# A hybrid decoder block: the carried attention state multiplied in 64-row pairs

## Chip, cores and metric

The kernel runs on one core of a Trainium2 chip. The metric is the time of one execution on the device in microseconds (us), the median of several runs. The profile comes from one more execution. Engines are called by these names: TensorE (PE in the profile, PEld for its weight loads), VectorE (DVE), ScalarE (ACT), GpSimd (POOL) and SyncE (SP), which issues the transfers. Matrix products land in PSUM, which has eight banks, of 512 fp32 values in each of 128 partitions.

## What is computed

One decoder layer over 2048 positions of width 1024: a norm, one input projection, two mixers side by side (gated linear attention with four heads, and a short gated convolution), an output projection with residual, a norm, a gated feed-forward part with residual, and a last norm. The change touches the attention alone. Per head, with q and k of width 64 and v of width 128:

```python
b = jnp.cumsum(log_a, axis=-2)
b_last = b[..., -1:, :]
q_i = q * jnp.exp(b)
k_i = k * jnp.exp(-b)
k_s = k * jnp.exp(b_last - b)
scores = jnp.einsum('nbhck,nbhsk->nbhcs', q_i, k_i)
scores = jnp.where(causal, scores, 0.0)
o_intra = jnp.einsum('nbhcs,nbhsv->nbhcv', scores, v)
chunk_kv = jnp.einsum('nbhsk,nbhsv->nbhkv', k_s, v)
...
o_inter = jnp.einsum('nbhck,nbhkv->nbhcv', q_i, state_prev)
o = o_intra + o_inter
```

`state_prev` is what all earlier chunks left: after each chunk the state is multiplied by the chunk's decay and `chunk_kv` is added. The output of each head is then normalised over its 128 values. The kernel takes chunks of 128 positions, 16 in all.

## The kernel before

Everything is laid out with features in partitions and positions along the free dimension. The positions are cut into four blocks `b` of 512, and two blocks make a half. The big products (`unit`, lines 332 to 370) work on a half at once in a scheme of seven block products instead of eight; each operand is split into a high and a low part (`split`, lines 145 to 147: ScalarE writes the high one, VectorE the difference), and each product of tiles is three matmuls (`product_step`, lines 328 to 330). One block product is 12 such matmuls into one bank.

The order of the body is: statistics and operands of the first half; input projection of half 0 (`in_proj`); the same of half 1; output projection of both halves (`out_proj`); the feed-forward part of both halves (`ffn_up`, `ffn_down`). The attention is a background job: a generator (`gla_half`, lines 578 to 598) that is put on a list when q, k, v and the gate of its half are projected, and that `tick` (lines 187 to 192) advances by one step behind every second block product. So the program text mixes attention steps between block products. The final order on each engine is then laid out by a planner ahead of the run, from estimated times, in priority of the program text: an instruction whose operands are late by the estimate lets later ones of its engine pass. On the chip each engine keeps the order so made and stands at an instruction whose operands are not there. The program's semaphores are put in by the same framework, and PSUM banks come from one pool of eight (`ps`, line 61), so a new tile waits until a bank is free.

One attention chunk (`b`, `t`) goes through four functions:

- `gla_load` (603 to 615) fetches k, q, decays, v and gate from scratch memory (SyncE issues 14 transfers), ScalarE takes two exponentials (609, 610) and VectorE multiplies them into `kq` (611, 612). `kq[:, 0:2]` holds the keys, `kq[:, 2:4]` the queries; in both, two heads `h = 2*i + e` share the 128 rows of pair `i`, head `e` in rows `64*e` to `64*e + 63`.
- `gla_scores` (617 to 639): four score matmuls of 64 rows, the two heads of a pair into two banks (622); VectorE copies them under the causal mask (625) to `scores`; TensorE transposes the keys into `kt_ps` (628) and the values into `v_ps` (631), ScalarE copies both out (632, 633); ScalarE scales the carried `state` by the chunk's decay `em` into `carry` (638), one head at a time.
- `gla_outputs` (641 to 676): for each head one matmul of scores and values (646) and one of queries and carry (648), added in one bank `o_ps`. The second one takes all 128 rows of the pair; `carry[:, h]` holds zeros in the other head's rows. Then chunk products `kv` of keys and values (653), VectorE's update of `state` (660 to 666), ScalarE's squares for the norm (670), VectorE's small steps (671, 155 to 158) and its scaling of the output (675).
- `gla_finish` (678 to 686) transposes the output (682), multiplies gain and gate (683), splits it and stores it.

In `gla_half` the steps follow each other as: scores of chunk n, finish of chunk n - 1, load of chunk n + 1, outputs of chunk n. The first chunk has no carry, and the last makes no `kv`.

Of the kernel before, what the change touches and what calls it, by code (L numbers as in the profile page):

```python
# [10 lines left out]
F32 = mybir.dt.float32  # L11
F32R = mybir.dt.float32r
U32 = mybir.dt.uint32
AF = mybir.ActivationFunctionType
ALU = mybir.AluOpType
# [3 lines left out]
P = 128  # L19
# [6 lines left out]
HEADS = 4  # L26
# [21 lines left out]
def tile_hymba_block(ctx, tc, x, xt, win, wa, wgu, wout, wffn, wdown, wdown_first, small, out):  # L48
    nc = tc.nc
    act, dve, pool, pe = nc.scalar, nc.vector, nc.gpsimd, nc.tensor  # L50

    def pool_of(name, bufs, **kw):
        return ctx.enter_context(tc.tile_pool(name=name, bufs=bufs, **kw))
# [7 lines left out]
    ps = pool_of("ps", 8, space=PSUM)  # L61
# [3 lines left out]
    mixer = mixing.enter_context(tc.tile_pool(name="mixer", bufs=1))  # L65
# [8 lines left out]
    mask = mixer.tile([P, 2, P], F32, name="mask")  # L74
# [12 lines left out]
    dve.memset(wa_sb[:, KD * 64 :].bitcast(F32), 0.0)  # L87
    scores = mixer.tile([P, HEADS, P], F32, name="scores")
    dve.memset(scores[:], 0.0)
    carry = mixer.tile([P, HEADS, P], F32, name="carry")  # L90
    dve.memset(carry[:], 0.0)
    state = [mixer.tile([P, P], F32, name=f"state{i}") for i in range(2)]
    halo = mixer.tile([P, 4, 2], F32, name="halo")
    dve.memset(halo[:], 0.0)
# [39 lines left out]
    def bt(name, shape=(P, PB)):  # L134
        return bx[0].tile(list(shape), F32, name=name, tag="b")
# [13 lines left out]
    def rsqrt(y, v, l, y0):  # L149

        act.activation(l, v, AF.Ln)
        act.activation(y0, l, AF.Exp, scale=-0.5)
        newton(y, v, l, y0)
# [298 lines left out]
    def build_h(later):  # L452


        def quad(k, j):
            return scaled(col(C_G1 + k), rbs[j], raws[j, k])

        return build_first(quad, first_weights, later)
# [119 lines left out]
    def gla_half(half):  # L578
        chunks = [(b, t) for b in (2 * half, 2 * half + 1) for t in range(PT)]
        with tc.issue_after(last_silu[0].ins):  # L580
            tables = act.preload_act_table_set("natural_log_exp_and_others")
        with tc.issue_after(tables.ins):
            nxt = gla_load(*chunks[0])
        o = None
        for n, (b, t) in enumerate(chunks):
            cur = nxt
            s = gla_scores(b, t, *cur)
            yield
            if o is not None:
                gla_finish(*chunks[n - 1], *o)  # L590
                yield
            if n + 1 < len(chunks):
                nxt = gla_load(*chunks[n + 1])
            o = gla_outputs(b, t, *s)
            yield
        gla_finish(b, t, *o)
        done.add((b, t))
        yield
# [16 lines left out]
        return kq, e, vt, g  # L615

    def gla_scores(b, t, kq, kt, v, g):
        sc = [ps.tile([P, 2, P], F32, name="sc", tag="mm") for _ in range(2)]
        for i in range(2):
            for e in range(2):  # L620
                r = slice(64 * e, 64 * e + 64)
                pe.matmul(sc[e][:, i, :], kq[r, i, :], kq[r, 2 + i, :], start=True, stop=True)
        smv = scores.rearrange("p (i e) c -> p e i c", e=2)
        for e in range(2):
            dve.copy_predicated(smv[:, e], mask[:].bitcast(U32), sc[e][:])
        kt_ps = ps.tile([P, 2, P], F32, name="kt_ps", tag="mm")
        for i in range(2):
            pe.transpose(kt_ps[:, i, :], kq[:, i, :], ident[:])
        v_ps = ps.tile([P, HEADS, P], F32, name="v_ps", tag="mm")
        for h in range(HEADS):  # L630
            pe.transpose(v_ps[:, h, :], v[:, h, :], ident[:])
        act.activation(kt[:, 0:2, :], kt_ps[:], AF.Copy)
        act.activation(v[:], v_ps[:], AF.Copy)
        if b or t:
            em = decays[b][0]
            for h in range(HEADS):
                i, r = h // 2, slice(64 * (h % 2), 64 * (h % 2) + 64)
                act.activation(carry[r, h, :], state[i][r, :], AF.Copy, scale=em[r, i, t : t + 1])
        return kq, kt, v, g

    def gla_outputs(b, t, kq, kt, v, g):
        first = b == 0 and t == 0
        _, dn, el = decays[b]
        o = ps.tile([P, HEADS, P], F32, name="o_ps", tag="mm")
        for h in range(HEADS):
            pe.matmul(o[:, h, :], scores[:, h, :], v[:, h, :], start=True, stop=first)
            if not first:
                pe.matmul(o[:, h, :], kq[:, 2 + h // 2, :], carry[:, h, :], start=False, stop=True)
        if b < NB - 1 or t < PT - 1:
            kv = ps.tile([P, 2, P], F32, name="kv", tag="mm")  # L650
            for i in range(2):
                for e in range(2):
                    pe.matmul(
                        kv[64 * e : 64 * e + 64, i, :], kt[:, i, 64 * e : 64 * e + 64],
                        v[:, 2 * i + e, :], start=True, stop=True,
                    )
            for i in range(2):
                last = el[:, i, t : t + 1]
                if first:
                    dve.tensor_scalar(state[i][:], kv[:, i, :], last, None, ALU.mult)  # L660
                else:
                    kvs = mtiny.tile([P, P], F32, name="kvs", tag="kvs")
                    dve.tensor_scalar(kvs[:], kv[:, i, :], last, None, ALU.mult)
                    dve.scalar_tensor_tensor(
                        state[i][:], state[i][:], dn[:, i, t : t + 1], kvs[:], ALU.mult, ALU.add
                    )
        ssq, l, y0 = [mtiny.tile([P, HEADS], F32, name=n, tag=n) for n in ("hsq", "hl", "hy")]
        sq = mtiny.tile([P, P], F32, name="sq", tag="rep")
        for h in range(HEADS):
            act.activation(sq[:], o[:, h, :], AF.Square, accum_out=ssq[:, h : h + 1])  # L670
        dve.tensor_scalar(ssq[:], ssq[:], 1.0 / P, EPS, ALU.mult, ALU.add)
        rsqrt(ssq[:], ssq[:], l[:], y0[:])
        osb = bt("osb", (P, HEADS, P))
        rs = ssq[:].rearrange("p (h c) -> p h c", c=1).to_broadcast([P, HEADS, P])
        dve.tensor_tensor(osb[:], o[:], rs, ALU.mult)
        return osb, g

    def gla_finish(b, t, osb, g):
# [27 lines left out]
    def build_mix(half):  # L706
        def pair(b, k):
            return load_pair(s_gla[b][:, k] if k < HEADS else s_mix[b][k - HEADS])

        return [[pair(2 * half + j, k) for j in range(2)] for k in range(KD)]  # L710
# [42 lines left out]
    def h2_first(ssq, ops):  # L753


        for _ in range(6):
            yield
        rb = []
        for j in range(2):
            rb.append(tiny.tile([P, PB], F32, name="rb2", tag="rb"))  # L760
            column_rstd(ssq[j], D, rb[j])
            yield

        def put(n, k, h):
            if n in LATER:
                store(s_h2[n][k][:], h[:])
            else:
                ops[n].append(split_op(h[:]))

        yield from combine(lambda k, j: s_x1[j][k][:], C_G2, rb, put)  # L770

    def h2_rest(ops):
        hs = deque()
        order = [(n, k) for n in LATER for k in range(4)]

        def fetch():
            if order:
                n, k = order.pop(0)
                h = bt("h")
                load(h[:], s_h2[n][k][:])  # L780
                hs.append((n, h))

        for _ in range(4):
            fetch()
        while hs:
            for _ in range(2):
                n, h = hs.popleft()
                ops[n].append(split_op(h[:]))
                fetch()
            yield  # L790
# [180 lines left out]
    ops, first = build_h(later)  # L971
# [10 lines left out]
    ssq = out_proj(0, build_mix(0))  # L982
    drain_background(lambda: (3, PT - 1) in done)
    h2 = no_operands()
    ssq = out_proj(1, build_mix(1), h2_first(ssq, h2), h2_rest(h2))
# [115 lines left out]
```

## Time and profile before

| what | us |
|---|---|
| median of three runs | 2149.33 |
| the three runs | 2149.33, 2143.01, 2150.7 |
| the profiled execution | 2146.09 |
| its span, first to last instruction | 2144.2 |
| attention chunks in the span, about | 305 to 700 |

The mean clock granted to TensorE was 0.989 of full speed. In the lines of the profile "L622" is line 622 of the kernel; a group of instructions is written as line, engine, operation, tiles written and read, shape, count, then busy time in us and the mean ns of one, then idle time of the engine ahead of it with the engine that ended it. A line of the timeline is start in us, duration, engine, line, operation, tiles, shape and count of merged instructions, with idle time ahead of it in brackets. A line of the waits is who waits, for whom, the us in total, the times, and the longest. A program matmul of two fp32 operands shows as two MATMUL instructions.

### The profile page before, as it was taken

The page shows a single profiled execution, that of the slowest core. Times are in us where ns is not written, and L with a number is a line of the kernel's source. Part 1 is how long each engine was busy: PE and PEld are TensorE (multiplying, and loading weights), DVE is VectorE, ACT ScalarE, POOL GpSimd, SP SyncE. Part 2 cuts the span into 40 slices and gives each one's busy share as a digit, 9 for nine tenths or more (in the row PEclk, how much of TensorE's full clock was granted, in tenths as well). Part 3 has the DMA queues.
Part 4 walks back from the last instruction along what each step waited for, and adds up shares of the span by engine and source line. Part 5 has one row for each costly group of instructions (what it writes and reads, how often), then busy time and mean ns, then how long its engine had stood idle before and what let it go on. Part 6 is the DMA issues. An engine that isn't in the chain of part 4 may idle for free.

```text
span 2144.2 us, 26906 instructions
## 1 busy us (share of the span) xinstructions
PE 2043.6 (95%) x9133; PEld 1651.3 (77%) x9133; DVE 1452.5 (68%) x2034; ACT 1012.1 (47%) x1962; POOL 997.0 (46%) x714
## 2 busy tenths in 40 slices
PE   4899899999999999999999999999999999999996
PEld 2677687887888887788888887787888888887775
DVE  8849965556774486888887664554686677664554
ACT  4555434574544235555454553333454454553344
POOL 4526422122201274655655436774644654445774
PEclk9999999999999999999999999999999999999998
DMA  4259658532577884465464577689455455487662
GB/s 150 76 199 315 218 228 286 156 125 79 166 247 256 309 294 152 167 240 220 172 237 182 185 303 283 254 336 355 157 191 205 154 197 196 172 329 293 266 265 108
DMA packets 189977, 467.64 MB, mean 218 GB/s; under 512 B 19856, under 2 KB 65168, under 8 KB 180112
## 3 DMA queue, kind: packets, MB, share of 16 engines
q1 hardware_dynamic: 189840, 465.93, 59.9%
q8 instruction: 72, 1.18, 0.2%
q14 instruction: 65, 0.53, 0.1%
HBM read 297.03 MB, written 168.82 MB: 217 GB/s over the span
## 4 chain that ended last, share of the span: by engine, by line
PE 70%; DVE 11%; DMA 8%; issue 4%; ACT 3%; POOL 3%; SPq 1%; DVEq 0%; POOLq 0%; ACTq 0%
PE mm L328 20%; PE mm L330 20%; PE mm L329 19%; DVE wq L147 3%; PE mm L722 3%; PE mm L725 3%; PE mm L723 3%; DMA raw<-in_wdown_dram 2%; DVE h L440 2%; DMA raw<-in_wffn_dram 1%; DVE so L147 1%; DVE op L147 1%; DMA op<-shT 1%; DVE c L352 1%; ACT wq L146 1%
## 5 line engine op out<-in xcount | busy, mean ns | idle before, releaser
L328 PE MATMUL mm<-op,wq 128*128 128x512 f32 x2495 | 982.1, 395 | 33.0 <-ACT c L348 20.3
L330 PE MATMUL mm<-op,wq 128*128 128x512 f32 x2495 | 967.6, 392 | 12.4 <-DVE wq L147 11.2
L329 PE MATMUL mm<-op,wq 128*128 128x512 f32 x2495 | 975.6, 391 | 2.5 <-DVE op L147 2.5
L147 DVE TENSOR_TENSOR wq<-raw,wq 128x512 fp32r<-128x512 f32 (+2 forms) x628 | 536.6, 860 | 320.2 <-ACT wq L146 318.3
L146 ACT ACTIVATE wq<-raw 128x512 fp32r<-128x512 f32 (+2 forms) x628 | 367.1, 589 | 566.7 <-PE mm L330 415.4
L328 PEld LDWEIGHTS mm<-op,wq 128*128 128x128 f32 x2495 | 470.4, 189 | 152.1 <-ACT c L348 27.1
L330 PEld LDWEIGHTS mm<-op,wq 128*128 128x128 f32 x2495 | 470.5, 189 | 121.9 <-DVE wq L147 22.4
L329 PEld LDWEIGHTS mm<-op,wq 128*128 128x128 f32 x2495 | 470.7, 189 | 99.8 <-DVE op L147 3.0
L313 POOL TENSOR_TENSOR raw<-s,raw 128x512 f32<-128x512 f32 (+2 forms) x98 | 130.7, 1333 | 437.7 <-DVE wq L147 403.1
L352 DVE TENSOR_TENSOR c<-mm,c 128x512 f32<-128x512 f32 x270 | 185.1, 686 | 100.1 <-PE mm L330 98.0
L311 POOL TENSOR_TENSOR s<-raw 128x512 f32<-128x512 f32 (+2 forms) x98 | 130.8, 1335 | 207.9 <-DMA raw<-in_wffn_dram 96.1
L318 POOL TENSOR_TENSOR raw<-raw 128x512 f32<-128x512 f32 (+2 forms) x98 | 130.4, 1331 | 129.5 <-DVE wq L147 128.9
L348 ACT ACTIVATE c<-mm 128x512 f32<-128x512 f32 x270 | 156.4, 585 | 23.8 <-PE mm L330 23.0
L704 POOL TENSOR_TENSOR ssx<-ssx,q 128x512 f32<-128x512 f32 x52 | 75.2, 1459 | 151.0 <-ACT q L703 151.0
L312 POOL TENSOR_TENSOR raw<-raw 128x512 f32<-128x512 f32 (+2 forms) x98 | 137.2, 1400 | 4.6
L884 POOL TENSOR_TENSOR y<-c,y 128x512 f32<-128x512 f32 x66 | 98.6, 1496 | 67.3 <-DVE c L352 67.2
L147 DVE TENSOR_TENSOR so<-t,so 128x512 fp32r<-128x512 f32 x100 | 89.6, 902 | 23.8 <-ACT so L146 23.6
L722 PE MATMUL mm<-op,wq 128*128 128x512 f32 x256 | 100.9, 394 | 0.0
L723 PE MATMUL mm<-op,wq 128*128 128x512 f32 x256 | 99.7, 390 | 0.0
L146 ACT ACTIVATE wq<-s 128x512 fp32r<-128x512 f32 (+2 forms) x98 | 57.6, 588 | 89.2 <-PE mm L330 86.6
L147 DVE TENSOR_TENSOR wq<-s,wq 128x512 fp32r<-128x512 f32 (+2 forms) x98 | 81.9, 835 | 15.6 <-ACT wq L146 15.2
L146 ACT ACTIVATE so<-t 128x512 fp32r<-128x512 f32 x100 | 62.9, 630 | 48.6 <-DMA sa_B<-so 19.9
(177 smaller groups left out, 1931.2 us busy)
## 6 DMA issues: line engine op xcount, KB each, us to landing
raw<-in_wffn_dram SPq DMA_DIRECT2D x44, 1024.0 KB, 6.1
sa_T<-so SPq DMA_DIRECT2D x88, 512.0 KB, 4.9
op<-sa_T SPq DMA_DIRECT2D x88, 512.0 KB, 9.6
sa_B<-so SPq DMA_DIRECT2D x69, 512.0 KB, 3.4
op<-sa_B SPq DMA_DIRECT2D x69, 512.0 KB, 9.2
raw<-in_win_dram SPq DMA_DIRECT2D x24, 1024.0 KB, 5.7
raw<-in_wdown_dram SPq DMA_DIRECT2D x24, 768.0 KB, 6.1
sx<-y SPq DMA_DIRECT2D x48, 256.0 KB, 3.4
```

The lines of the kernel that those rows point to most:

```text
L146: last_hi[:] = [act.activation(hi, src, AF.Copy)]
L147: return dve.tensor_tensor(lo, src, hi.bitcast(F32), ALU.subtract)
L311: pool.tensor_tensor(s1, a21, a22, ALU.add)
L312: pool.tensor_tensor(a21, a11, a21, ALU.subtract)
L313: pool.tensor_tensor(a11, s1, a11, ALU.subtract)
L328: pe.matmul(o[:], wh, xh, start=first and k == 0, stop=False, skip_group_check=True)
L329: pe.matmul(o[:], wh, xl, start=False, stop=False, skip_group_check=True)
L330: return pe.matmul(o[:], wl, xh, start=False, stop=k == n - 1, skip_group_check=True)
L348: act.activation(t[:], o[:], AF.Copy)
L352: dve.tensor_tensor(t[:], o[:], t[:], ALU.add)
L722: pe.matmul(o[e, j][:], wh, m[:, 0, :], start=k == 0, stop=False)
L723: pe.matmul(o[e, j][:], wh, m[:, 1, :], start=False, stop=False)
```

## The change

The carry has one tile of two pairs instead of four heads, with no zero rows and so no memset. It is scaled with one ScalarE instruction for a pair. Queries and carry are multiplied in the 64 rows of the head. The outputs of the two heads of a pair go to two banks, `o[0]` and `o[1]`, the first using columns 0 to 255 of it. To save banks, the transposed keys `kt_ps` go into the right half of the scores' first bank, and `kv` goes into the right half of `o[0]`. In each pair both score products come first, then both carry products. The scaling of the output becomes two instructions, one for each bank.

```diff
-    carry = mixer.tile([P, HEADS, P], F32, name="carry")
-    dve.memset(carry[:], 0.0)
+    carry = mixer.tile([P, 2, P], F32, name="carry")
...
-        sc = [ps.tile([P, 2, P], F32, name="sc", tag="mm") for _ in range(2)]
+        sc = [ps.tile([P, HEADS, P], F32, name="sc", tag="mm") for _ in range(2)]
+        kt_ps = sc[0][:, 2:4, :]
...
-            dve.copy_predicated(smv[:, e], mask[:].bitcast(U32), sc[e][:])
-        kt_ps = ps.tile([P, 2, P], F32, name="kt_ps", tag="mm")
+            dve.copy_predicated(smv[:, e], mask[:].bitcast(U32), sc[e][:, 0:2, :])
...
-        act.activation(kt[:, 0:2, :], kt_ps[:], AF.Copy)
+        act.activation(kt[:, 0:2, :], kt_ps, AF.Copy)
...
-            for h in range(HEADS):
-                i, r = h // 2, slice(64 * (h % 2), 64 * (h % 2) + 64)
-                act.activation(carry[r, h, :], state[i][r, :], AF.Copy, scale=em[r, i, t : t + 1])
+            for i in range(2):
+                act.activation(carry[:, i, :], state[i][:], AF.Copy, scale=em[:, i, t : t + 1])
...
-        o = ps.tile([P, HEADS, P], F32, name="o_ps", tag="mm")
-        for h in range(HEADS):
-            pe.matmul(o[:, h, :], scores[:, h, :], v[:, h, :], start=True, stop=first)
-            if not first:
-                pe.matmul(o[:, h, :], kq[:, 2 + h // 2, :], carry[:, h, :], start=False, stop=True)
+        o = [ps.tile([P, HEADS, P], F32, name="o_ps", tag="mm") for _ in range(2)]
+        for i in range(2):
+            for e in range(2):
+                h = 2 * i + e
+                pe.matmul(o[e][:, i, :], scores[:, h, :], v[:, h, :], start=True, stop=first)
+            for e in range(2):
+                r = slice(64 * e, 64 * e + 64)
+                if not first:
+                    pe.matmul(
+                        o[e][:, i, :], kq[r, 2 + i, :], carry[r, i, :], start=False, stop=True
+                    )
...
-            kv = ps.tile([P, 2, P], F32, name="kv", tag="mm")
+            kv = o[0][:, 2:4, :]
...
-            act.activation(sq[:], o[:, h, :], AF.Square, accum_out=ssq[:, h : h + 1])
+            act.activation(
+                sq[:], o[h % 2][:, h // 2, :], AF.Square, accum_out=ssq[:, h : h + 1]
+            )
...
-        rs = ssq[:].rearrange("p (h c) -> p h c", c=1).to_broadcast([P, HEADS, P])
-        dve.tensor_tensor(osb[:], o[:], rs, ALU.mult)
+        for e in range(2):
+            rs = ssq[:].rearrange("p (i e c) -> p e i c", e=2, c=1)[:, e].to_broadcast([P, 2, P])
+            dst = osb[:].rearrange("p (i e) c -> p e i c", e=2)[:, e]
+            dve.tensor_tensor(dst, o[e][:, 0:2, :], rs, ALU.mult)
```

## The prediction

> **What bounds the kernel now.** I read the page first (shares by engine, the chain that ended last), then busy time by stretch, then the waits of the one stage that the diff touches, and at last its instructions in order of time. The page:
>
> ```profile
> span 2144.2 us, 26906 instructions
> PE 2043.6 (95%) x9133; PEld 1651.3 (77%) x9133; DVE 1452.5 (68%) x2034; ACT 1012.1 (47%) x1962; POOL 997.0 (46%) x714
> PE 70%; DVE 11%; DMA 8%; issue 4%; ACT 3%; POOL 3%; SPq 1%; DVEq 0%; POOLq 0%; ACTq 0%
> ```
>
> TensorE is busy 95% of the span and carries 70% of the chain that ended last. The profiled execution took 2146.1 us, 1.9 around its span; the three plain runs have a median of 2149.33, 3.2 above it, and lie between 2143.0 and 2150.7. Sums below are made against 2146.1. About 0.5%, 10.7 us, is what a measurement of this kernel can tell from no change.
>
> The attention chunks (16, of which 15 have a carried state) run from 305 to 700 us, between the projections' products. Busy time by stretch, columns PE, PEld, DVE, ACT, POOL, clock, DMA:
>
> ```profile
> 305.00:480.00 175.00, 171.28 (x911) 140.58 (x910) 104.02 (x199) 99.73 (x237) 37.98 (x28) 0.98 0.61 210
> ...
> 535.00:700.00 165.00, 164.53 (x896) 135.99 (x897) 105.94 (x225) 79.24 (x211) 23.92 (x16) 1.00 0.66 218
> ```
>
> In the two stretches with chunks TensorE is idle 3.7 of 175 and 0.5 of 165 us. So a microsecond of TensorE's order there is a microsecond of the end, and one of VectorE (about 60% busy) or ScalarE (about 50%) is not, unless TensorE stands for it. TensorE's own waits there (us, times, longest):
>
> ```profile
> PE sc L622 <- issue: 3.7, 1, 3.7
> PE sc L622 <- DVE kq L612: 1.9, 1, 1.9
> PE mm L328 <- ACT c L348: 1.2, 1, 1.2
> ```
>
> Nothing waits for a carry (L638) or for the normalised output. What the change can win is TensorE's issue time; what it can lose is a new stand of TensorE.
>
> **The row pairs.** A program matmul of fp32 is two instructions in the trace (x2). One chunk's output block:
>
> ```profile
> 404.79 0.40 PE L330 MATMUL mm<-op,wq 128*128 128x512 f32 x1
> 405.02 0.39 PE L646 MATMUL o_ps<-vt,scores 128*128 128x128 f32 x2
> 405.24 0.39 PE L648 MATMUL o_ps<-carry,kq 128*128 128x128 f32 x2
> ...
> 406.58 0.39 PE L648 MATMUL o_ps<-carry,kq 128*128 128x128 f32 x2
> 406.90 0.66 PE L653 MATMUL kv<-vt,ee 128*64 128x128 f32 x8
> ```
>
> The block takes 406.90 - 405.02 = 1.88 us: 16 instructions 0.11 apart (405.24 - 405.02, halved), the last one 0.21 before the column-split kv. What 64-row pairs cost is seen in the scores, which are written in this way already:
>
> ```profile
> 370.95 0.39 PE L330 MATMUL mm<-op,wq 128*128 128x512 f32 x1
> 371.26 0.71 PE L622 MATMUL sc<-kq 64*128 64x128 f32 x8
> 371.91 0.44 PE L628 MATMUL kt_ps<-ident,kq 128*128 128x128 f32 x2
> 372.19 0.60 PE L631 MATMUL v_ps<-ident,vt 128*128 128x128 f32 x4
> ```
>
> and, over all chunks, least, median and greatest duration of one such instruction:
>
> ```profile
> L622 PE MATMUL sc<-kq x128: 272/272/580, 305.2 to 673.7; 64*128 64x128 f32 x128
> ```
>
> Eight instructions end 0.71 us after the first began. One takes 0.272, so eight starts lie within 0.44 us, four steps of 0.11: two heads run beside each other. The first comes 0.31 behind the last product, where the full-row block above comes 0.23 behind its own (404.79 to 405.02): entering costs 0.08; leaving costs 0.21 (371.91 less the last start, 371.70) where full rows are 0.11 apart.
>
> The changed block does for each of two pairs: four full instructions (three steps, 0.33), entry 0.11 + 0.08 = 0.19, two steps of paired rows (one gap, 0.11), exit 0.21: 0.84 us. Twice that is 1.68 against 1.88, 0.20 a chunk, 15 chunks: **3.0 us less**. Bounds: if the new pairs did not overlap, each would need 0.22 more, 1.68 + 0.44 - 1.88 = +0.24 a chunk, +3.6 us. If switching were free, 12 steps of 0.11 and the last exit's extra 0.10 make 1.42, -6.9 us. I keep -3.0, since operands, banks and order of heads are those of the scores row. The Trainium skill, in TensorEngine Tiling (Array Packing), section Key Properties, says that a change of tiling mode drains TensorE; it speaks against a block that changes mode four times where it changed once. The trace agrees, with its 0.08 and 0.10: by this rule the sum is the -3.0, without it the -6.9.
>
> **ScalarE and VectorE.**
>
> ```profile
> L638 ACT ACTIVATE carry<-state,em 64x128 f32<-64x128 f32 x60 | 24.1, 401 | 2.7 <-DVE state L664 2.0
> L675 DVE TENSOR_TENSOR osb<-o_ps,hsq 128x512 f32<-128x512 f32 x16 | 11.0, 690 | 0.5
> L625 DVE COPY_PREDICATED scores<-mask,sc 128x256 f32<-128x256 uint32 x32 | 13.6, 442 | 2.8 <-PE sc L622 2.6
> L663 DVE TENSOR_SCALAR kvs<-kv,el 128x128 f32<-128x128 f32 x28 | 8.5, 345 | 9.1 <-PE kv L653 9.1
> ```
>
> ```profile
> ACT wq L146 <- PE mm L330: 77.5, 46, 3.9
> ACT ee L632 <- PE kt_ps L628: 7.7, 8, 3.7
> ```
>
> Four scalings become two over all 128 rows. Even at the old 0.401 us each this frees 30 x 0.401 = 12.0 us of ScalarE. Its worth is nothing: no TensorE instruction waits for it, and ScalarE waits for TensorE there more than for anything else (77.5 us). The one 512-wide scaling of the output becomes two of 256; by the nearest 256-wide PSUM reader, 0.442, that is 2 x 0.442 - 0.690 = 0.19 more, 3.1 us of VectorE in 16 chunks. It is hidden beside products while 40% of VectorE is idle; uncovered, it is 3.1. The dropped memset of the carry is one VectorE instruction of 512 values, 0.69 if it is priced like the output's; it lies where VectorE has no loaded data yet, 0.
>
> kv now lies in the bank of o[0]. TensorE writes both in its own order, so it gains no wait. ScalarE's squares of o[0] come behind kv (0.66, row 406.90) and, if the two readers are kept apart, behind VectorE's two readings of it (0.345 each): 1.35 us a chunk, up to 20 us of ScalarE. Behind them in ScalarE's order stand weight splits; these run ahead of TensorE (the same 77.5 us), and I cost this at nothing. Without that lead it is up to 20. Per chunk seven banks become six, but two are held until the output is scaled where one was. TensorE's waits for banks in this stage are the 1.2 us above: 0, at most once more 1.2. No transfer is moved, and the queues of SP and POOL hold the same work.
>
> **The new wait.** The transposes of k now go into the right half of the scores' first bank, while VectorE's masked copy reads its left half. Are the two kept apart? The trace shows that this program orders a bank as a whole. By 382.80 three heads of an output bank are done, the fourth follows at 385.60 behind a product, and ScalarE, idle for 2.90 us before 385.57, squares the first head only after the fourth:
>
> ```profile
> 382.41 0.39 PE L648 MATMUL o_ps<-carry,kq 128*128 128x128 f32 x2
> 385.60 0.39 PE L648 MATMUL o_ps<-carry,kq 128*128 128x128 f32 x2
> 385.57 0.63 ACT L146 ACTIVATE wq<-raw 128x512 fp32r<-128x512 f32 x1 [2.90 <-PE mm L330]
> 386.59 0.27 ACT L670 ACTIVATE sq<-o_ps 128x128 f32<-128x128 f32 x1
> ```
>
> So I take it that the transposes wait for the copy. Behind them on TensorE stand v's transposes, if these are not put first, and the next products; ScalarE's copy of k waits for them (7.7 us, above), then kv. How late the copy comes, in the first, a quick, a slow and the last of 16 chunks (the quick one's scores are quoted above):
>
> ```profile
> 305.24 0.71 PE L622 MATMUL sc<-kq 64*128 64x128 f32 x8
> 307.07 0.45 DVE L625 COPY_PREDICATED scores<-mask,sc 128x256 f32<-128x256 uint32 x1
> ...
> 372.01 0.45 DVE L625 COPY_PREDICATED scores<-mask,sc 128x256 f32<-128x256 uint32 x1
> ...
> 547.38 0.71 PE L622 MATMUL sc<-kq 64*128 64x128 f32 x8
> 550.86 0.43 DVE L625 COPY_PREDICATED scores<-mask,sc 128x256 f32<-128x256 uint32 x1
> ...
> 673.28 0.71 PE L622 MATMUL sc<-kq 64*128 64x128 f32 x8
> 675.47 0.78 DVE L625 COPY_PREDICATED scores<-mask,sc 128x256 f32<-128x256 uint32 x2
> ```
>
> From the scores' end to the end of the first copy it is 1.6, 0.5, 3.2 and 1.9 us in these; the 16 sum to 22.9. V's four transposes fill 0.44 of each (four steps of 0.11), which leaves 15.9: the upper bound, with nothing else put between. The lower bound is 0, since the order is laid out ahead and products can go between, as between the heads above. What such laying out leaves uncovered is told by two rows. Products wait for ScalarE to clear their bank, a wait of this kind: 20.3 us over the kernel behind 270 copies, 0.075 each, 1.2 for 16 (both lines below).
>
> ```profile
> PE mm L328 <- ACT c L348: 20.3, 15, 4.4
> L348 ACT ACTIVATE c<-mm x270: 575/582/611, 67.1 to 2099.8; 128x512 f32<-128x512 f32 x135
> ```
>
> The scores wait for VectorE's kq in the same step of the same 16 chunks: 3.7 + 1.9 = 5.6 us (the 3.7 is put down to "issue"; I count it as VectorE's, where the scores' operands come from, and without it the price is 1.9). These rows are the nearest in engine and place: **+5.6**.
>
> **The sum:** 2146.1 - 3.0 + 5.6 = 2148.7; **I forecast 2149 us**. It is 2.6 above the profiled execution and level with the median, a difference inside the spread of the plain runs.
>
> **Rivals.** (a) Slower: TensorE stands at the transposes of k until the masked copy has ended, with nothing put between: 2146.1 - 3.0 + 15.9 = **2159**. It decides from a mean stand of 0.86 us a chunk (13.7 / 16), where the loss passes 10.7. For it: the slow copies above. Against it: products stand between the steps of a chunk already. The Trainium skill, in PSUM — Partial Sum Buffer, section PSUM bank collisions raise a hardware error, has a rule that asks for this wait: two engines may not touch one bank in the same partitions at once, disjoint columns included. The squares' rows agree with an order by bank; a collision itself is in no run here. (b) Faster: the order, laid out anew from the first chunk on with a freer ScalarE, closes the 5.6 before the scores and the waits of the first products behind the chunks (700 to 900 us):
>
> ```profile
> PE mm L330 <- DVE wq L147: 5.6, 2, 3.2
> PE mm L328 <- DVE c L352: 2.0, 1, 2.0
> ```
>
> That is 2146.1 - 3.0 - 5.6 - 7.6 = **2130**. Against it: these waits are for VectorE, which the change gives more to do. (c) The change does not do what it says: the new pairs do not overlap, 2146.1 + 3.6 + 5.6 = **2155**. Against it stands the scores' 0.44 us.
>
> **How the numbers follow.** Forecast 0.50, (a) 0.24, (b) 0.16, (c) 0.10. The forecast and (c) are within 0.5% of the median (2138.6 to 2160.1): so same 0.60, faster 0.16, slower 0.24; (a) is 13 us, 0.6%, above its own base and counts as slower. With these chances 0.2 may stay outside: the range takes in (a), moved up by the 3.2 between profiled execution and median, and goes about half the way from the forecast to (b): 2138 to 2163. It holds each bound of an unknown cost taken alone (2139 for free switching with no wait, 2159 for the full stand), but not the 20 us of held squares, which ScalarE's lead speaks against.
>
> **What would show it.** Right: the carry's eight instructions in 64-row form, each four within about 0.4 us; outputs' block near 1.7 us; the transposes of k behind the masked copy, with TensorE's idle before them under 6 us in all; ScalarE's carry group near 12 us for 30. Wrong: idle before them over 13 us (a); an output block over 1.9 (c); a gain that lies outside 305 to 700 us (b), where the order was laid out anew and no step of mine has a price.

## The result and the profile after

The changed kernel takes **2156.48 us** (median of 13 runs, 2150.39 to 2160.8). The kernel before, run beside it, takes 2148.70 (13 runs, 2143.01 to 2150.7). The ratio is 1.0037, with a 95% interval of 1.0026 to 1.0047: slower by about 8 us. The forecast of 2149 was 7.5 us too low. The range held the time, which is partly luck: as told below, the two main terms of the sum were wrong by 8.6 and 5.6 us, in opposite directions. The profiled execution took 2152.36 us.

The page of the changed kernel (span, busy time by engine, chain by engine):

```profile
span 2150.5 us, 26915 instructions
PE 2053.2 (95%) x9133; PEld 1650.2 (77%) x9133; DVE 1451.1 (67%) x2049; ACT 995.5 (46%) x1932; POOL 997.0 (46%) x714
PE 69%; DVE 11%; DMA 11%; ACT 3%; issue 3%; POOL 2%; SPq 1%; DVEq 0%; ACTq 0%; POOLq 0%
```

TensorE runs as many matmuls as before (9133), and they take 9.6 us more. ScalarE lost 16.6 us and gave nothing for it. Busy time by stretch in the changed kernel:

```profile
305.00:480.00 175.00, 170.48 (x909) 135.92 (x908) 102.97 (x208) 91.32 (x222) 37.52 (x28) 1.00 0.62 211
...
535.00:700.00 165.00, 162.65 (x859) 129.32 (x860) 106.32 (x230) 69.87 (x195) 23.18 (x16) 1.00 0.64 214
```

Read the counts in brackets behind PE. In the second stretch, at full clock in both, TensorE was busy for 162.65 us against 164.53, but got through 859 matmuls against 896. Of the 37 that are missing, each worth some 0.2 us, the 1.9 us of idle time explain about a quarter; the rest is slower work (33 of the 37 are big products, so the mix of large and small matmuls is not the reason). (The first stretch hides this: 911 against 909, but the clock before was 0.98 there. Why is told at the end.)

TensorE's waits in the chunks' stage of the changed kernel (who, for whom, us, times, longest):

```profile
PE sc L622 <- DVE kq L611: 5.6, 2, 3.7
PE ot L690 <- DVE osb L683: 2.0, 2, 1.2
PE mm L327 <- ACT c L347: 1.2, 1, 1.2
```

The waits of the scores and products are the same in sum as before. New are 2.0 us of the output's transposes (L690). At the keys' transposes, where I had put 5.6 us, there is none.

One chunk's output block in the changed kernel, in order of time:

```profile
403.37 0.40 PE L329 MATMUL mm<-op,wq 128*128 128x512 f32 x1
403.60 0.61 PE L646 MATMUL o_ps<-vt,scores 128*128 128x128 f32 x4
404.14 0.49 PE L650 MATMUL o_ps<-carry,kq 64*128 64x128 f32 x4
404.56 0.71 PE L646 MATMUL o_ps<-vt,scores 128*128 128x128 f32 x4
405.21 0.49 PE L650 MATMUL o_ps<-carry,kq 64*128 64x128 f32 x4
405.63 0.66 PE L657 MATMUL o_ps<-vt,ee 128*64 128x128 f32 x8
```

The block takes 405.63 - 403.60 = **2.03 us**, against 1.88 before and 1.68 in the forecast. The pairs do overlap. A narrower stretch of the same timeline tells the single steps:

```profile
404.14 0.38 PE L650 MATMUL o_ps<-carry,kq 64*128 64x128 f32 x2
404.36 0.28 PE L650 MATMUL o_ps<-carry,kq 64*128 64x128 f32 x2
404.56 0.60 PE L646 MATMUL o_ps<-vt,scores 128*128 128x128 f32 x3
```

Two instructions begin together at 404.14, two at 404.36, and full rows come back at 404.56. The three rows of 404.56 end at 405.16; with 0.275 each the last began at 404.89, so the second, 0.11 earlier, at 404.78. So the starts are 0.20 (into the pairs), 0.21 (to the next pair), 0.20 (out) and 0.21 (to the second full instruction) apart, and only then 0.11 again. (By form I mean the rows and columns that stand in a matmul's line: 128*128, 64*128 or 128*64.) **A change of form costs two steps of about 0.2 us where the stream has 0.11: 0.2 us in all.** The weight loads of the same stretch (PEld) show the same from their side:

```profile
403.72 0.30 PEld L646 LDWEIGHTS o_ps<-vt,scores 128*128 128x128 f32 x2
404.14 0.30 PEld L650 LDWEIGHTS o_ps<-carry,kq 64*128 64x128 f32 x4
404.56 0.52 PEld L646 LDWEIGHTS o_ps<-vt,scores 128*128 128x128 f32 x4
```

In the stream a load begins one step ahead of its matmul: the loads at 403.72 and 403.83 serve the matmuls at 403.83 and 403.94. At a change it does not. The first load of the new form begins with its matmul (404.14, 404.56), and the second follows 0.11 later, so the second matmul too comes late.

The order as the planner laid it out makes it worse where heads alternate. One chunk does so throughout (540.30), another for its first pair of heads (693.9):

```profile
540.08 0.38 PE L627 MATMUL sc<-ident,kq 128*128 128x128 f32 x2
540.30 0.39 PE L646 MATMUL o_ps<-vt,scores 128*128 128x128 f32 x2
540.61 0.48 PE L650 MATMUL o_ps<-carry,kq 64*128 64x128 f32 x2
541.03 0.49 PE L646 MATMUL o_ps<-vt,scores 128*128 128x128 f32 x2
...
543.53 0.50 PE L327 MATMUL mm<-op,wq 128*128 128x512 f32 x1
```

Here each head changes the form twice, nothing runs beside anything, and from the block's first start to the next product (540.30 to 543.53) it takes 3.23 us.

**The books of the stage.** All kernels of this study run the same products, and ahead of the attention stage and behind it in the same order (inside it some change places), so I cut each trace at the same two of them (the 937th and the 2341st product instruction, 297 and 713 us in the kernel before, 298 and 721 in the changed one) and split TensorE's time between. "Work" is the sum of steps from one start to the next without idle time, half-clock stretches counted at full clock; "idle" is time with no matmul running; "changes" are the places where the next matmul has another number of rows or columns; "breaks" are the places where an attention instruction follows a product. Ahead of the stage the work is the same within 2.1 us in all kernels, behind it within 1.7. The kernel before ran beside each round of experiments, and its median moved by 1.0 us between them; so kernels of different rounds are best compared by their ratios, and times in us that are taken from ratios are marked so.

| kernel | changes | breaks | work | idle | median | ratio to before, 95% |
|---|---|---|---|---|---|---|
| before | 72 | 65 | 405.5 | 7.2 | 2147.7 to 2148.7 | 1 |
| changed | 133 | 82 | 414.1 | 8.8 | 2156.48 | 1.0026 to 1.0047 |
| e1_full_rows | 78 | 84 | 408.3 | 11.1 | 2162.13 | 1.0042 to 1.0081 |
| e2_own_banks | 132 | 71 | 413.0 | 7.0 | 2153.08 | 1.0014 to 1.0045 |
| e3_rows_together | 101 | 82 | 407.4 | 10.0 | 2152.01 | 1.0005 to 1.0034 |
| e4_head_by_head | 183 | 81 | 429.0 | 8.8 | 2172.68 | 1.0094 to 1.0136 |
| e5_full_own | 76 | 71 | 407.4 | 7.0 | 2148.09 | 0.9995 to 1.0018 |
| e6_together_own | 102 | 71 | 406.8 | 7.0 | 2147.62 | 0.9990 to 1.0009 |
| e7_carry_first | 72 | 64 | 400.8 | 8.4 | 2143.41 | 0.9974 to 1.0002 |
| e9_keys_own_bank | 137 | 79 | 414.8 | 8.4 | 2158.40 | 1.0032 to 1.0064 |
| e10_kv_own_bank | 131 | 85 | 413.6 | 4.4 | 2152.27 | 1.0010 to 1.0035 |
| e11_full_keys_own | 82 | 74 | 408.7 | 8.5 | 2150.45 | 1.0002 to 1.0034 |

The change adds 8.6 us of work and 1.7 of idle time. A fit over these profiles and the repeat of before gives work = 386.6 + 0.199 x changes + 0.074 x breaks - 5.2 where carry rows run in pairs, and leaves at most 0.4 us in any of them. No experiment changes the breaks alone, so their price stands on this fit only. By it the 8.6 are 61 x 0.199 = 12.1 for changes, 17 x 0.074 = 1.3 for breaks, less 5.2 that the pairs win.

### The profile page after: what moved, and what is told of

It reads as the page before. It is cut to its first block, busy times and chain, and to the rows that moved or that the text cites. A ratio compares the mean times of both kernels' runs of the same rounds, so it can differ in the third digit from the quotient of the medians.

```text
span 2150.5 us, 26915 instructions
## 1 busy us (share of the span) xinstructions
PE 2053.2 (95%) x9133; PEld 1650.2 (77%) x9133; DVE 1451.1 (67%) x2049; ACT 995.5 (46%) x1932; POOL 997.0 (46%) x714
## 4 chain that ended last, share of the span: by engine, by line
PE 69%; DVE 11%; DMA 11%; ACT 3%; issue 3%; POOL 2%; SPq 1%; DVEq 0%; ACTq 0%; POOLq 0%
PE mm L327 20%; PE mm L329 20%; PE mm L328 20%; DVE wq L146 2%; DMA raw<-in_wdown_dram 2%; DVE h L439 2%; PE mm L730 2%; PE mm L733 2%; PE mm L731 2%; DMA op<-sa_B 1%; DMA op<-siT 1%; DVE op L146 1%; DVE so L146 1%; DMA op<-shT 1%; SPq L137 1%
## 5 line engine op out<-in xcount | busy, mean ns | idle before, releaser
L329 PEld LDWEIGHTS mm<-op,wq 128*128 128x128 f32 x2495 | 471.1, 189 | 118.5 <-DVE wq L146 19.4
```

The lines of the kernel that those rows point to most:

```text
L329: return pe.matmul(o[:], wl, xh, start=False, stop=k == n - 1, skip_group_check=True)
```

## The experiments

Theories: **M**, changes of form at 0.2 us each are the loss; **M2**, the same after the first four kernels, with 0.2 us a change, about 0.09 a break, up to 0.11 won for each paired instruction, and nothing else. The rivals put the loss elsewhere: the shared banks, the second output bank, the new wait, or the forecast's own price of 0.08 to 0.10 a change. The first four expectations count 8 changes fewer in each kernel (64 in before, 125 in the changed one) than the table; the later ones count as the table does. All edits are to the changed kernel, and the diffs are cut to their core.

**e1_full_rows.** The carry in four heads with zero rows again, banks and order of the change kept.

```diff
-            for i in range(2):
-                act.activation(carry[:, i, :], state[i][:], AF.Copy, scale=em[:, i, t : t + 1])
+            for h in range(HEADS):
+                i, r = h // 2, slice(64 * (h % 2), 64 * (h % 2) + 64)
+                act.activation(carry[r, h, :], state[i][r, :], AF.Copy, scale=em[r, i, t : t + 1])
...
-                        o[e][:, i, :], kq[r, 2 + i, :], carry[r, i, :], start=False, stop=True
+                        o[e][:, i, :], kq[:, 2 + i, :], carry[:, h, :], start=False, stop=True
```

> The changed kernel with the carry multiplied in all 128 rows again (zero rows beside each head, four scalings); two output banks, shared banks, the two-part output scaling and the order of heads stay. Theory M (each change of TensorE's row or column form costs about 0.2 us, a drain and a weight load that nothing hides): TensorE's order has 70 changes of form instead of 125 (64 before), the 6 us are gone, ratio to before 1.000 to 1.002, an output block of 1.9 us. Rival B (banks held longer, the new wait at the transposes of k, more VectorE work): the loss stays, ratio 1.003 to 1.004.

It took 2162.13 us (6 runs), ratio 1.0061 [1.0042, 1.0081]: every theory missed. Its work fell by 5.8 us as M wants (78 changes, 408.3), but its idle time is the highest, 11.1, and it spent more time at half clock. So its work and its time do not go together: against the changed kernel it has less work and takes longer. TensorE's waits in the stage of e1:

```profile
PE sc L623 <- DVE kq L612: 5.5, 2, 3.7
PE ot L692 <- DVE osb L685: 2.8, 2, 1.9
PE sc L623 <- issue: 1.6, 1, 1.6
PE mm L328 <- ACT c L348: 1.2, 1, 1.2
```

So full rows do not save the change while the banks stay shared. Something in the sharing costs, too.

**e2_own_banks.** Pairs kept, both shared tiles in banks of their own.

```diff
-        kt_ps = sc[0][:, 2:4, :]
+        kt_ps = ps.tile([P, 2, P], F32, name="kt_ps", tag="mm")
...
-            kv = o[0][:, 2:4, :]
+            kv = ps.tile([P, 2, P], F32, name="kv", tag="mm")
```

> The changed kernel with the transposed keys and the chunk product kv in banks of their own again; the 64-row carry stays. TensorE's order has 124 changes of form, as many as the change. Theory M: the loss stays, ratio to before 1.003 to 1.004, output blocks of 2.02 us. Rival B, in its part on shared banks and the wait for the masked copy: ratio 0.999 to 1.001.

2153.08, 1.0029 [1.0014, 1.0045]. Most of the loss stays without any sharing, as M has it: work 413.0, breaks 71, idle 7.0. The gain on the changed kernel (1.7 us by the ratios, 3.4 by the medians) is not apart from it by the intervals.

**e3_rows_together.** The score products of all four heads first, then the four carry products: two changes fewer in a block. `start` is set on the first product of each bank only.

```diff
-                pe.matmul(o[e][:, i, :], scores[:, h, :], v[:, h, :], start=True, stop=first)
-            for e in range(2):
-                r = slice(64 * e, 64 * e + 64)
-                if not first:
+                pe.matmul(
+                    o[e][:, i, :], scores[:, h, :], v[:, h, :], start=i == 0, stop=first,
+                    skip_group_check=True,
+                )
+        if not first:
+            for i in range(2):
+                for e in range(2):
+                    r = slice(64 * e, 64 * e + 64)
```

> The changed kernel with all four score products of a chunk first and all four 64-row carry products behind them (only the first matmul in each of the two banks clears it), so that a full block enters and leaves the 64-row form once: 93 changes of form instead of 125. Theory M: an undivided block takes about 1.61 us (seven steps of 0.11, entry 0.20, then 0.21, 0.11, 0.11, exit 0.20) where the change takes 2.02 and before 1.88; the whole 2147, ratio to before 0.998 to 1.000. Rival B: nothing but the order of eight matmuls differs, ratio 1.003 to 1.004.

2152.01, 1.0020 [1.0005, 1.0034]. The block is what was expected, in time order:

```profile
400.24 1.06 PE L646 MATMUL o_ps<-vt,scores 128*128 128x128 f32 x8
401.23 0.71 PE L654 MATMUL o_ps<-carry,kq 64*128 64x128 f32 x8
401.88 0.66 PE L662 MATMUL o_ps<-vt,ee 128*64 128x128 f32 x8
```

1.64 us, less than before's 1.88: eight carry instructions within 0.65. Work fell by 6.7 us with 32 changes. But the kernel is still slower than before, and M alone had it even or faster: 82 breaks and 10.0 us of idle time remain. This gave M2 its second price.

**e4_head_by_head.** The opposite: score and carry product of each head in turn, so that every chunk has the order of 540.30 us.

```diff
-                pe.matmul(o[e][:, i, :], scores[:, h, :], v[:, h, :], start=True, stop=first)
-            for e in range(2):
                 r = slice(64 * e, 64 * e + 64)
+                pe.matmul(o[e][:, i, :], scores[:, h, :], v[:, h, :], start=True, stop=first)
                 if not first:
```

> The changed kernel with score product and 64-row carry product in turn, head by head, so that no two heads pair and the form changes at every step: 175 changes of form instead of 125 (64 before). Theory M at 0.2 us a change: a block of 8 x 0.41 = 3.3 us, 15 chunks about 20 us over before, 2169, ratio 1.009 to 1.010. The price of my prediction (0.08 and 0.10 a change): a block of 2.5 us, about 10 us over before, ratio 1.004 to 1.005.

2172.68 (6 runs), 1.0115 [1.0094, 1.0136], at M and far above what the forecast's price allows. Its timeline:

```profile
406.78 0.39 PE L647 MATMUL o_ps<-vt,scores 128*128 128x128 f32 x2
407.09 0.49 PE L649 MATMUL o_ps<-carry,kq 64*128 64x128 f32 x2
407.51 0.49 PE L647 MATMUL o_ps<-vt,scores 128*128 128x128 f32 x2
...
410.01 0.33 PE L656 MATMUL o_ps<-vt,ee 128*64 128x128 f32 x2
```

3.23 us for the block; two instructions and the change to the next two take 0.42, of which 0.22 are the two steps of a stream. Against e1, same breaks within three, 105 more changes bring 20.7 us of work: 0.197 each. This settles the price.

**e5_full_own.** e1 and e2 together: of the change only the second output bank with its readers, and the scaling of the output in two, remain.

```diff
-        kt_ps = sc[0][:, 2:4, :]
+        kt_ps = ps.tile([P, 2, P], F32, name="kt_ps", tag="mm")
...
-                        o[e][:, i, :], kq[r, 2 + i, :], carry[r, i, :], start=False, stop=True
+                        o[e][:, i, :], kq[:, 2 + i, :], carry[:, h, :], start=False, stop=True
...
-            kv = o[0][:, 2:4, :]
+            kv = ps.tile([P, 2, P], F32, name="kv", tag="mm")
```

> The changed kernel without its 64-row carry and without its shared banks: carry in all 128 rows with zero rows and four scalings, keys' transposes and kv in banks of their own; two output banks, two-part output scaling and order of heads stay. TensorE's order has 71 interruptions of the product stream and 76 changes of form in the chunk stage (before 65 and 72, the change 82 and 133). Theory M2 (0.2 us a change of form, about 0.09 us an interruption, 0.11 us won for each paired instruction, nothing else): 1.3 us over before in TensorE's work, ratio 0.999 to 1.002. Rival (the second output bank, held until the output is scaled, or VectorE's extra instruction costs by itself): ratio 1.003 or more.

2148.09, 1.0006 [0.9995, 1.0018]: level with before. The second bank and VectorE's extra instructions cost nothing that can be measured. And this is the clean price of the rows: e2 differs from e5 in the rows and their scaling alone, and has 5.6 us more work and 4.9 more time by the ratios (the two intervals overlap a little). The other two pairs of this kind agree in work: 6.1 (e9 against e11), 5.8 (changed against e1); in time only the first of them does, since e1 is slow for another reason.

**e6_together_own.** e3 with both tiles in banks of their own.

```diff
-        kt_ps = sc[0][:, 2:4, :]
+        kt_ps = ps.tile([P, 2, P], F32, name="kt_ps", tag="mm")
...
+                pe.matmul(
+                    o[e][:, i, :], scores[:, h, :], v[:, h, :], start=i == 0, stop=first,
+                    skip_group_check=True,
+                )
...
-            kv = o[0][:, 2:4, :]
+            kv = ps.tile([P, 2, P], F32, name="kv", tag="mm")
```

> The third experiment (four score products, then four 64-row carry products) with the keys' transposes and kv in banks of their own: 71 interruptions, 102 changes of form, all 60 pairs but a few. Theory M2: +0.5 + 5.9 - 6.4, TensorE's work in the stage equal to before's, ratio 0.999 to 1.001. Rival, that sharing banks costs nothing and the third experiment's 1.002 is all from elsewhere: ratio 1.002.

2147.62, 0.9999 [0.9990, 1.0009]: pairs laid out well and banks apart give back all of the loss, and no gain.

**e7_carry_first.** If a change is what costs, put the carry products beside rows that are 64 high already: the carry is scaled one step earlier, its products are issued right ahead of the scores, in the same form, and the scores are held behind them. Banks apart.

```diff
+        if b or t:
+            for i in range(2):
+                for e in range(2):
+                    r = slice(64 * e, 64 * e + 64)
+                    last = pe.matmul(
+                        o[e][:, i, :], kq[r, 2 + i, :], carry[r, i, :], start=i == 0, stop=False,
+                        skip_group_check=True,
+                    )
+        with ExitStack() as stack:
+            if b or t:
+                stack.enter_context(tc.issue_after(last.ins))
...
+                    pe.matmul(
+                        sc[e][:, i, :], kq[r, i, :], kq[r, 2 + i, :], start=True, stop=True
+                    )
```

> The carry products go ahead of the chunk's score products, which are in 64-row form too and are held behind them, so that the carry adds no change of form of its own; the carry is scaled one step earlier, and the keys' transposes and kv have banks of their own. 64 interruptions and 72 changes of form, as before (65 and 72), and all 60 pairs. Theory M2: 6.6 us less of TensorE's work in the stage than before, ratio 0.996 to 0.998. Rival, that pairing itself wins nothing on the chip or that the output banks held from the scores on make TensorE wait: ratio 1.000 or more.

2143.41, 0.9988 [0.9974, 1.0002]: the fastest of the study, some 10 us under the changed kernel, and under before by 2.6 us by the ratio (4.2 by the medians), which the interval doesn't settle; the expectation was more, 0.996 to 0.998. Its timeline shows the carry for 0.55 us and no change of form behind it:

```profile
409.17 0.39 PE L327 MATMUL mm<-op,wq 128*128 128x512 f32 x1
409.49 0.71 PE L633 MATMUL o_ps<-carry,kq 64*128 64x128 f32 x8
410.04 0.61 PE L643 MATMUL sc<-kq 64*128 64x128 f32 x8
410.58 0.44 PE L650 MATMUL kt_ps<-ident,kq 128*128 128x128 f32 x2
```

Changes are back at 72, breaks at 64, and work is 4.7 us under before. So the 64-row carry can win work where it adds no change of form; that the whole gets faster by it is likely, not shown.

**e8_before_again.** The kernel before, profiled once more, for the error of one profile.

> The kernel before, profiled once more. If TensorE's work at full clock is a matter of the order of its instructions alone, it repeats within 0.5 us in the stage of the chunks (405.5 us) and behind it (1382.5 us), while the number and place of the windows of half clock differ and move the total by some microseconds.

One run, 2144.95 us. The work of the stage repeats within 0.01 us (405.48 both times), that behind it within 0.2; idle time is 7.65 against 7.15. So differences of a microsecond in work are real; the plain times of single runs are not that good.

**e9_keys_own_bank** and **e10_kv_own_bank.** One of the two shared tiles each.

```diff
-        kt_ps = sc[0][:, 2:4, :]
+        kt_ps = ps.tile([P, 2, P], F32, name="kt_ps", tag="mm")
```

> The changed kernel with a bank of its own for the transposed keys alone; kv stays in the output's bank. 79 interruptions and 137 changes of form in the chunk stage (the change 82 and 133, with both banks apart 71 and 132). Theory M2, by these counts: TensorE's work in the stage as in the change, 414 to 415 us, ratio to before 1.003 to 1.004; sharing costs only where it splits TensorE's order. Rival, the forecast's new wait (transposes of the keys behind the masked copy) carries the 3.4 us between the change and the kernel with both banks apart: ratio 1.002 to 1.003, idle of TensorE in the stage back from 8.8 to 7.0 us.

```diff
-            kv = o[0][:, 2:4, :]
+            kv = ps.tile([P, 2, P], F32, name="kv", tag="mm")
```

> The changed kernel with a bank of its own for kv alone; the transposed keys stay in the scores' bank. 85 interruptions and 131 changes of form. Theory M2, by these counts: work in the stage near 414 us, ratio to before 1.003 to 1.004. Rival, kv in the output's bank (squares and scaling behind VectorE's reading, later output transposes) carries the loss of sharing: ratio 1.002 to 1.003 and no wait for the output transposes, which were 2.0 us in the change.

Keys alone: 2158.40 (7 runs), 1.0048 [1.0032, 1.0064], no better than the change, so the new wait is not the loss. Chunk state (`kv`) alone: 2152.27 (12 runs), 1.0023 [1.0010, 1.0035], 3.0 us better by the ratios, and as good as both apart. Here M2 missed the time, since it prices no idle time, and its rival had both the ratio and the missing wait right. ScalarE's squares (L674) in the changed kernel and then in e10 (busy, mean ns, idle ahead of them and for whom):

```profile
L674 ACT ACTIVATE sq<-o_ps 128x128 f32<-128x128 f32 x64 | 17.4, 272 | 27.5 <-DVE kvs L667 22.9 <-PE o_ps L650 4.0
```

```profile
L674 ACT ACTIVATE sq<-o_ps 128x128 f32<-128x128 f32 x64 | 17.8, 278 | 19.1 <-PE o_ps L650 17.6
```

With `kv` in the output's bank the squares wait 22.9 us for VectorE's readings of `kv`; apart, they wait for TensorE alone. Behind them come the norm, the scaling (L683) and the output's transposes. TensorE's waits in the stage of e10:

```profile
PE mm L327 <- ACT c L347: 2.4, 2, 1.2
PE sc L622 <- DVE kq L611: 1.9, 1, 1.9
```

The 2.0 us of the transposes are gone, and 3.7 of the scores' wait as well; idle falls to 4.4 us. The 3.7 can't be put down to `kv`: e2, e5 and e6 have `kv` in a bank of its own too, and keep a gap of 3.7 us there. The work did not change (413.6). The intervals of the two kernels overlap, so the waits carry the reading more than the times do. They are of one profile each, but the other kernels agree: the six that share `kv`'s bank, the changed one among them, have 19.4 to 35.5 us of the squares' wait for VectorE's readings, and 0.8 to 2.8 us of the transposes' wait; those with `kv` apart show none of the first and at most 0.4 of the second.

**e11_full_keys_own.** e1 with the keys in a bank of their own, `kv` still shared.

```diff
-        kt_ps = sc[0][:, 2:4, :]
+        kt_ps = ps.tile([P, 2, P], F32, name="kt_ps", tag="mm")
...
-                        o[e][:, i, :], kq[r, 2 + i, :], carry[r, i, :], start=False, stop=True
+                        o[e][:, i, :], kq[:, 2 + i, :], carry[:, h, :], start=False, stop=True
```

> The first experiment (128-row carry, zero rows) with a bank of its own for the transposed keys; kv stays in the output's bank. 74 interruptions and 82 changes of form. Theory M2: 2.7 us over before in TensorE's work, 408 us in the stage, ratio 1.001 to 1.002 with idle near 7 us. The first experiment, with the same work, took 1.006 at more windows of half clock; if sharing the keys' bank makes these by idle time, they go here, and if sharing kv's bank does, the ratio stays over 1.004.

2150.45, 1.0018 [1.0002, 1.0034], as M2 has it. So the excess of e1, 9.2 us by the ratios (11.7 by the medians), goes with the keys in the scores' bank, though the same sharing costs nothing beside paired rows (e2 and e10 are level). In e1's stage I find 2.6 us of it as idle time. Most of the rest is half-clock time: the two profiled spans differ by 13.1 us, and TensorE ran at half clock for 72.2 us in e1 and for 51.4 in e11. **Why full rows and shared keys together give that order stays open.**

## Why the prediction was wrong, step by step

**TensorE sets the end, and a microsecond of its order is a microsecond of the time: right.** The profiled execution is 6.3 us longer; the stage between the two cuts is 7.1 us longer, the time ahead of it 0.9, and the time behind it 1.7 shorter.

**"The row pairs ... 3.0 us less": this step failed.** It was +5.6 (work, e2 against e5). I had each change at 0.08 in and 0.10 out; it is 0.20 both ways. The mechanism stood in the sum, with less than half its price. The error is one of counting. Eight score instructions start within 0.44 us, and I read "four steps of 0.11". Four pairs have three gaps, so the mean gap is 0.146. The trace of before had it; a stretch of 0.1 us shows it:

```profile
371.26 0.49 PE L622 MATMUL sc<-kq 64*128 64x128 f32 x4
371.70 0.28 PE L622 MATMUL sc<-kq 64*128 64x128 f32 x2
```

The four that were begun by then end at 371.75; with 0.27 or 0.28 for the last, the second pair began at 371.47, 0.21 behind the first, and the next ones at 0.11. With the steps measured above the block adds up to 1.99 us (three steps of 0.11, 0.205, 0.206, 0.202, 0.213, two of 0.11, 0.205, 0.206, 0.202); 2.03 were measured. The Trainium skill says in TensorEngine Tiling (Array Packing), section Key Properties, that changing the tiling mode drains TensorE; the trace agrees, and adds that the second weight load behind the change comes late as well, which doubles the price that I took from the first step alone.

**What I did not count: changes outside of the block.** Three more a chunk in 15 chunks are 45; the trace has 61. The planner's order brought the other 16: one and a half blocks head by head (540.30 and 693.9), which make 6 of them, and attention instructions that stand singly between products. I took the order of the program text for the order on the engine.

**The new wait, +5.6: wrong, it measured 0.** The transposes do stay behind the masked copy, but the planner put products between. TensorE, then VectorE's copies, in one chunk of the changed kernel:

```profile
369.61 0.71 PE L622 MATMUL sc<-kq 64*128 64x128 f32 x8
370.25 0.66 PE L630 MATMUL v_ps<-ident,vt 128*128 128x128 f32 x4
370.67 0.47 PE L327 MATMUL mm<-op,wq 128*128 128x512 f32 x1
```

```profile
370.35 0.45 DVE L625 COPY_PREDICATED scores<-mask,sc 128x256 f32<-128x256 uint32 x1
...
371.96 0.43 DVE L625 COPY_PREDICATED scores<-mask,sc 128x256 f32<-128x256 uint32 x1
```

The keys follow only at 375.11, and in each of the 16 chunks at least 1.3 us behind the end of the first copy. Instead of a stand the products are broken more often: 17 breaks more in the stage, 1.3 us by the fit. Not all of them are the keys': with the keys apart (e9) 79 breaks stay, and only with both tiles apart (e2) 71. My two terms made +2.6 together; the runs put +5.6 in the rows, 0 in the wait, and some 2 to 4 us by the ratios in breaks and idle time that come with the shared banks.

**ScalarE: right.** The carry's group fell by 12 us, and TensorE had no wait there that this could have shortened:

```profile
L636 ACT ACTIVATE carry<-state,em 128x128 f32<-128x128 f32 x30 | 11.8, 397 | 0.9 <-DVE state L668 0.6
```

**VectorE, the second bank: right.** The scaling rose from 11.0 to 12.1 us, by 1.1 instead of 3.1, and e5 shows no cost.

**`kv` in the bank of `o[0]` at nothing: wrong, by a few us.** I had bounded the held squares at 20 us of ScalarE; they measured 22.9. But I looked at the splits behind them only. The chain from the squares to the output's transposes ends on TensorE (2.0 us of wait). By the ratios the sharing costs 3.0 (changed against e10), 4.1 (e9 against e2) and 2.6 us (e11 against e5); in each of the three the two intervals overlap, but all have one sign. The transposes' wait is 0.8 us in e9 and in e11, so it is a part of the cost; what the rest is stays open.

**The rivals.** (a) was refuted by the waits. (b) had the right place, the order laid out anew, and the wrong sign: 82 breaks for 65. (c) gave 2155, the nearest to 2156.48, and its sign came true, a block over 1.9 us; yet the pairs do overlap. My sign could not tell pairs that don't overlap from changes that are dear. The single starts can.

## What to carry to other kernels

Before tiling rows in pairs, count the changes of form on the engine's real order and price one from single starts, not from a mean over a group: here it is 0.2 us, and two fp32 products of 128 columns beside each other save 0.17 (by the fit) to 0.22 us (two steps). So one such pair between full rows, with a change on either side, loses about 0.2; two pairs together come out about even (e6); best put such products next to others of the same form (e7). In this program the readers of two tiles in one PSUM bank wait for each other: follow that wait through to the engine that sets the end. A wait that you fear on a planned engine may come back as a changed order instead, so compare orders before stalls.

## What the runs showed of the hardware beside this

TensorE's clock is halved for 3.4 us or a multiple of it behind some idle gaps. Both kernels have a gap of 3.7 us in front of the scores near 345 us. The same stretch, before and then changed (PEclk is the third number from the end):

```profile
347.00:354.00 7.00, 6.58 (x24) 5.50 (x25) 1.10 (x3) 0.98 (x2) 0.33 (x2) 0.51 0.95 255
```

```profile
347.00:354.00 7.00, 5.51 (x33) 4.60 (x34) 2.91 (x5) 1.72 (x3) 1.16 (x1) 1.00 0.97 292
```

Before, 24 matmuls at a clock of 0.51; changed, 33 at full clock. Of the 12 profiles with this gap, 11 have a half-clock stretch behind it; why the changed kernel's has none is not shown. In the repeat of before it lasts 3.4 us instead of 6.8. A gap of 1.9 us near 533 us was followed by one in 4 of 13. The mean clock goes with most of the spread between runs: among runs of one kernel the time falls by about 1.5 us for each 0.001 of mean clock. It is why the stage's work, at full clock, is the better measure here, and why the profiled difference (6.3 us) is smaller than work and idle time together (10.3): 3.2 us of half clock in the stage fell on before alone. The Trainium skill, in TensorE: Matmul & The Clock Gate, Part 1: The HAM clock gate (the "warmup" mystery), tells of a free-running window of some 3.4 us, and of half clock after at least one idle window. The length agrees; but the gap of 1.9 us, shorter than a window, was followed by half clock in four of these traces.
